# Padding between the split ffn inputs in their pool, and one parameter tile moved to another pool

## The chip, the cores and the metric

The kernel runs on one core of one Trainium2 chip. Its time is the device time of one execution in microseconds (us). A core has a matrix engine (TensorE; PE in the profile, with its weight loads as PEld), three engines for elementwise work (VectorE, DVE; ScalarE, ACT; GpSimd, POOL), a queue engine (SyncE, SP) and DMA engines that move data between the main memory and the on-chip memory. On-chip memory (SBUF) has 128 partitions; a tile takes the same byte range in each partition, and this text speaks of addresses as bytes within a partition. Matmul results go to PSUM tiles of at most 512 float32 columns.

## The reference

Two layers over 1024 latent tokens and 256 context tokens, model width 1024, all float32. Each layer is a mixer and a channel mixer (ffn), each behind a modulated RMS norm and with a gated residual. The mixer of layer 0 is attention beside a convolution, that of layer 1 a recurrent scan in both directions. What the change touches are the inputs of the last two products of each layer:

```python
def swiglu(h, w1, w3, w2):
    return (jax.nn.silu(h @ w1) * (h @ w3)) @ w2
...
        h_lat = h_lat + g1_l * o_lat
        f_lat = rms_norm(h_lat, norm_ffn[i]) * (1 + sc2_l) + sh2_l
        h_lat = h_lat + g2_l * swiglu(f_lat, ffn_w1[i], ffn_w3[i], ffn_w2[i])
        if not last:
            h_ctx = h_ctx + g1_c * o_ctx
            f_ctx = rms_norm(h_ctx, norm_ffn[i]) * (1 + sc2_c) + sh2_c
            h_ctx = h_ctx + g2_c * swiglu(f_ctx, ffn_w1[i], ffn_w3[i], ffn_w2[i])
```

`o_lat` is the output of the mixer, itself a product with a 1024 by 1024 matrix (`even_w_out`, `rw_wo`). The ffn's hidden width is 2816, and context tokens go through it in layer 0 only.

## The kernel before

**Split products.** Every large product is done in three matmuls of float32r, a float32 format that TensorE reads at one pass: an operand is split into a rounded part (`hi`) and the rest (`lo`), and `mm3` (line 57) adds `wh·xh`, `wh·xl` and `wl·xh` on lines 59, 60 and 61. In a call to matmul the second argument is the stationary operand (128 by 128, loaded into the array by a weight load) and the third is the moving one (128 by up to 512 columns). A weight load of the next matmul goes on while the matmul before it streams its moving operand.

**Tokens.** They are tiled as `TT`: 256 context tokens (tile 0) and two tiles of 512 latent tokens (1 and 2). In layer 1 only two tiles of 512 remain (0 and 1).

**The split inputs.** `operands` (line 1446) opens a pool `X0` or `X1` on the left side of SBUF and puts into it, tile after tile, `xh` and `xl`: eight blocks (kb) of 128 features, each a run of 256 or 512 tokens. Layer 0 has the order 1, 0, 2 and layer 1 the order 0, 1. The same tiles serve twice: first they hold the split output of the mixer, which `mix_out` (line 680) multiplies with the output projection into PSUM tiles `pw`; then `norm_split` writes the split input of the ffn into them.

**The ffn** (line 718) runs over 22 blocks of 128 hidden features in groups of two. For each block and token tile, two PSUM tiles `pf` (for w1 and w3) take 8 × 3 = 24 matmuls each, moving `xh`/`xl` past the stationary `whi`/`wlo`. The product of the two goes, split again, to `gh`/`gl`, and then eight PSUM tiles `pf2` for each token tile take 2 × 3 = 6 matmuls, moving `gh`/`gl` past the rows of w2, which lie in tiles of the same names `whi`/`wlo`. ACT and DVE split the weights (lines 54 and 55) and finish the results (lines 750, 751 and 762) meanwhile.

**Where tiles lie.** Pools on the left stack upwards, with the pool `G` of constants and parameters at the bottom (its last byte is at 22,176 before the change); pools with `side="right"` stack downwards from the top of the partition. A pool's tiles lie in the order in which they are made. Added up from the tile sizes, before the change:

| tile | pool, side | address | mod 512 |
|---|---|---|---|
| `ah` (inputs of layer 0's projections `pg`, `pz`) | A0, left | 22,176 | 160 |
| `whi` for them | W0, left | 108,192 | 160 |
| `xh1`, `xh0`, `xh2`, layer 0 | X0, left | 22,176, 54,944, 71,328 | 160 |
| `whi`, layer 0 projection and ffn | WX0 and FW0, right | 155,616 and 151,520 | 480 |
| `gh`, layer 0 | FW0, right | 112,608 | 480 |
| `xh0`, `xh1`, layer 1 | X1, left | 42,080, 74,848 | 96 |
| `wyh0` (first two blocks of layer 1's projection) | WY, left, above X1 | 110,688 | 96 |
| `whi`, layer 1 projection and ffn | WX1 and FW1, right | 156,576 and 152,480 | 416 |
| `gh`, layer 1 | FW1, right | 119,712 | 416 |

The `lo` tiles and the further buffers lie whole multiples of 512 bytes away from these; so do the kb blocks (2048 bytes of `xh` for 512 tokens, 1024 for 256; 512 of `whi`). A pool that is opened over a closed one reuses its bytes, and its first writers wait for the last readers of the old tiles below them.

**X1 opens early.** `prepared` (line 1484) opens X1 while the scan of layer 1 still runs, in the place of the scan's preparation pool (`prep`), loads six of the eight blocks of each x tile through `o` (`layer1_in`, line 1408), and starts the projection's first two output blocks with the early weights `wyh`/`wyl`.

**`rt`** is a tile of 128 by 128 (512 bytes) into which `params` (line 108) collects parameter rows, group by group (A, B, C, M), before a transposition puts them into `parA` to `parM`. It lies in `G`, with one buffer. T0 is the right-hand pool of the first stage, closed when the inputs are normed; T1, also on the right, takes its place later with `zq2`.

Of the kernel before, what the change touches and what calls it, by code (L numbers as in the profile page):

```python
# [9 lines left out]
F32 = mybir.dt.float32  # L10
F32R = mybir.dt.float32r
# [6 lines left out]
P = 128  # L18
D = 1024
KB = D // P  # L20
# [19 lines left out]
def f32(ap):  # L40
    return ap.bitcast(F32)


class Kern:
# [60 lines left out]
        self.Wr = None  # L105
        self.acc = {}

    def params(self, *groups):

        nc, tc, I = self.nc, self.tc, self.I  # L110
        rows = {
            "A": ["c", "c_ctx", "ada_b", "norm_mix"],
            "B": ["mla_q_norm", "mla_kv_norm", "conv_b", "conv_ln_g", "conv_ln_b", "rw_k_k", "rw_k_a",
                  "rw_w0", "rw_a0", "rw_r_k", "rw_ln_g", "rw_ln_b", "norm_ffn"],
            "C": ["conv_w"],
            "M": ["rw_mu"],
        }
        for g in groups:
            rt = self.G.tile([P, P], F32, tag="rt", name="rt", bufs=1)
            nc.vector.memset(rt, 0.0)  # L120
            r = 0
            where = {}
            for nm in rows[g]:
                a = I[nm]
                n = int(np.prod(a.shape)) // P
                sh = list(a.shape)
                if len(sh) == 1:
                    a2 = a.rearrange("(b p) -> b p", p=P)
                elif len(sh) == 2:
                    a2 = a.rearrange("a (b p) -> (a b) p", p=P)  # L130
                elif len(sh) == 3:
                    a2 = a.rearrange("a c (b p) -> (a c b) p", p=P)
                elif nm == "rw_r_k":
                    a2 = a.rearrange("a c (h e) d -> (a c h) (e d)", e=2)
                else:
                    a2 = a.rearrange("a c e (b p) -> (a c e b) p", p=P)
                (nc.sync if g == "A" else nc.gpsimd).dma_start(rt[r:r + n, :], a2)
                where[nm] = (r, n)
                r += n
            ps = self.psM.tile([P, 512], F32, tag="m", name="ps")[:, :P]  # L140
            nc.tensor.transpose(ps, rt, self.ident)
            ct = self.G.tile([P, P], F32, tag="par" + g, name="par" + g)
            nc.vector.tensor_copy(ct, ps)
            for nm, (r, n) in where.items():
                self.par[nm] = ct[:, r:r + n]
            if g == "A":
                nc.scalar.activation(self.silc[:, :, 0], self.par["c"], AF.Silu)
                nc.scalar.activation(self.silc[:, :, 1], self.par["c_ctx"], AF.Silu)
# [95 lines left out]
    def layer0_mix(self):  # L244
# [6 lines left out]
        with ExitStack() as st:  # L251
            pool = lambda s, **k: s.enter_context(tc.tile_pool(reuse_waits="tile", **k))
# [5 lines left out]
            A = pool(left, name="A0", bufs=1)  # L258
# [3 lines left out]
            self.W, self.wraw, self.wbuf = W, 1, 2  # L262

            with tc.tile_pool(name="T0", bufs=1, side="right", reuse_waits="tile") as tp:
                self.params("A")
                xs = []
                ss = tp.tile([P, NTK], F32, name="ss")

                def load(b, q):
                    x = tp.tile([P, D], F32, tag="xin" if b < 2 else "araw", name="xin", bufs=2 if b < 2 else 18)  # L270
                    r = b * P
                    q.dma_start(x, I["ctx"][0][r:r + P] if r < NCTX else I["x"][0][r - NCTX:r - NCTX + P])
                    xs.append(x)

                def rms(b0, b1):
                    for b in range(b0, b1):
                        sq = tp.tile([P, D], F32, tag="sq", name="sq", bufs=1)
                        nc.scalar.activation(sq, xs[b], AF.Square, accum_out=ss[:, b:b + 1])
                    r = ss[:, b0:b1]
                    nc.scalar.activation(r, r, AF.Sqrt, bias=self.eps, scale=1.0 / D)  # L280
                    nc.vector.reciprocal(r, r)
                    for b in range(b0, b1):
                        nc.vector.tensor_scalar(xs[b], xs[b], ss[:, b:b + 1], None, op0=ALU.mult)

                for b in range(2):
                    load(b, nc.sync)
                for _ in self.ada(0, 0, 2, tp, 18, psO, psM):
                    pass
                w0 = [self.load_w(w_in[:, c0:c0 + P]) for c0 in (544, 1056)]
                for b in range(2, NTK):  # L290
                    load(b, nc.sync)
                rms(0, 2)
                self.gains(0, 0)
                for t0, n in TT:
                    if t0:
                        rms(t0 // P, (t0 + n) // P)
                    for g in {256: "BC", 768: "M"}.get(t0, ()):
                        self.params(g)
                    s = int(t0 == 0)
                    for fb in range(KB):  # L300
                        ps = psM.tile([P, 512], F32, tag="m", name="tps")
                        for i in range(n // P):
                            nc.tensor.transpose(ps[:, i * P:(i + 1) * P], xs[t0 // P + i][:, fb * P:(fb + 1) * P], self.ident)
                        t = tp.tile([P, 512], F32, tag="nt", name="nt", bufs=3)
                        nc.scalar.activation(t[:, :n], ps[:, :n], AF.Identity, scale=self.gs[:, 0, 0, s, fb:fb + 1], bias=self.mod[0][:, fb, s:s + 1])
                        hi = ah[:, fb, t0:t0 + n]
                        nc.gpsimd.tensor_scalar(hi, t[:, :n], 1.0, 0.0, op0=ALU.mult, op1=ALU.add)
                        nc.vector.tensor_tensor(al[:, fb, t0:t0 + n], t[:, :n], f32(hi), op=ALU.subtract)
# [68 lines left out]
            with tc.tile_pool(name="T1", bufs=1, side="right", reuse_waits="tile") as tp:  # L377
                ada = self.ada(0, 2, 6, tp, 3, psO, psM)
                for j in range(4):
# [5 lines left out]
                    g = self.par["mla_q_norm" if j < 2 else "mla_kv_norm"][:, j % 2:j % 2 + 1]  # L385
# [252 lines left out]
            for i in range(NH):  # L638
# [11 lines left out]
                for j, _ in enumerate(attend(i)):  # L650
                    for sd in side:
                        g, n, a, b, d = sd
# [784 lines left out]
    def run(self):  # L1437
        tc = self.tc
        pool = lambda s, **k: s.enter_context(tc.tile_pool(reuse_waits="tile", **k))
        with ExitStack() as st:  # L1440
# [5 lines left out]
            def operands(l, sizes):  # L1446
                X = pool(xs, name=f"X{l}", bufs=1)
                order = (0, 1) if l else (1, 0, 2)
                xs_ = {i: [X.tile([P, KB, sizes[i]], F32R, name=f"x{k}{i}") for k in "hl"] for i in order}
                xh, xl = ([xs_[i][k] for i in range(len(sizes))] for k in range(2))  # L1450
                return order, xh, xl, pool(ps, name=f"pX{l}", bufs=5, space=PSUM)

# [23 lines left out]

            sizes = [n for _, n in TT]
            hT = phase(0, sizes, operands(0, sizes), self.layer0_out)
            LR = pool(rs, name="LR", bufs=1)
            self.layer1_proj(hT, hs.close, LR)  # L1480
            nn.close()
            sizes, x = [512, 512], []

            def prepared():
                x.extend(operands(1, sizes))
                _, xh, xl, psum = x
                self.x1 = xh, xl
                Y = pool(ys, name="WY", bufs=1)
                self.wy = []

                def load(mb):
                    w = [Y.tile([P, KB, P], F32R, name=f"wy{k}{mb}") for k in "hl"]
                    for k0, k1 in ((0, 6), (6, 8)):
                        raw = self.wyr[:, :k1 - k0]
                        self.nc.sync.dma_start(raw, self.I["rw_wo"][0][k0 * P:k1 * P, mb * P:(mb + 1) * P].rearrange("(k p) m -> p k m", p=P))
                        self.split(w[0][:, k0:k1], w[1][:, k0:k1], raw)
                    self.wy.append(w)

                self.wyr = Y.tile([P, 6, P], F32, name="raw")
                load(0)  # L1500
                with tc.tile_pool(name="TY", bufs=1, reuse_waits="tile") as tp:
                    self.layer1_in(xh, xl, tp)
                yield
                Y = pool(ys, name="WZ", bufs=1)
                load(1)
                for mb in range(2):
                    w = self.wy[mb]
                    for ti in range(2):
                        ps = self.acc[mb, ti] = psum.tile([P, 512], F32, tag="mm", name="pw")
                        for kb in range(6):  # L1510
                            self.mm3(ps, w[0][:, kb], w[1][:, kb], xh[ti][:, kb], xl[ti][:, kb], kb == 0, False)
                            if kb % 3 == 2:
                                yield
# [55 lines left out]
```

## Time and profile before

| | us |
|---|---|
| three runs, median (lowest to highest) | 4186.94 (4185.19 to 4190.39) |
| the profiled execution | 4188.13 |
| its span, first to last instruction | 4186.4 |
| TensorE busy | 3832.1 |
| DVE busy | 2403.9 |
| ACT busy | 1741.1 |
| POOL busy | 1161.3 |

The profile is of one execution. "PE" rows are matmuls and "PEld" rows weight loads, which overlap them; matmuls are pipelined, so the duration of one (from its start to its modelled end) is longer than the step from one start to the next. The granted clock is the share of TensorE's full clock that the chip allowed at the time. Names stand without their trailing numbers: `xh0`, `xh1` and `xh2` are all `xh`, and `gh` is the source that tells `pf2` from `pf`.

### The profile page before, as it was taken

To read this page: it belongs to the slowest core of one execution; us is meant where nothing else is said; L and a number is where in the kernel's file an instruction comes from. 1 tells how busy PE (TensorE), PEld (TensorE's weight loads), DVE (VectorE), ACT (ScalarE), POOL (GpSimd) and SP (SyncE) were. 2 spreads that over 40 slices of the span, in tenths; PEclk is the share of its full clock that TensorE was granted. 3 is DMA by queue.
4 is the path that set the end of the run, shared out by engine and by line. 5 is a ranking of instruction groups with operands and counts; after the bars stand their busy time and mean duration, and the time that the engine had idled before them with its cause. 6 is when DMAs were issued, how large, how long until landed. Compare 5 with 4: busy or idle time off the path is not lost. (4 is left out here: it accounts for less than half of the span.)

```text
span 4186.4 us, 70705 instructions
## 1 busy us (share of the span) xinstructions
PE 3832.1 (92%) x28764; PEld 3132.3 (75%) x28764; DVE 2403.9 (57%) x4577; ACT 1741.1 (42%) x3590; POOL 1161.3 (28%) x978
## 2 busy tenths in 40 slices
PE   8888899899999999997998979787887799999999
PEld 5665667688888888886887957676776578888887
DVE  5698776555333433338678378878787654333433
ACT  4446566643111111116667357666666442111111
POOL 2869554510000000004223164645544020000000
PEclk9898999999999999998999979898988899999999
DMA  4322222331111111113223222222222231111111
GB/s 174 125 86 69 74 92 72 109 109 46 41 39 33 40 41 41 36 36 99 74 95 102 79 85 70 80 70 78 75 62 65 85 111 51 46 45 51 51 46 56
DMA packets 301669, 297.07 MB, mean 71 GB/s; under 512 B 19408, under 2 KB 267872, under 8 KB 301344
## 3 DMA queue, kind: packets, MB, share of 16 engines
q1 hardware_dynamic: 293488, 277.07, 21.4%
q10 hardware_dynamic: 7056, 14.75, 1.0%
q8 instruction: 227, 3.72, 0.4%
q0 software_dynamic: 800, 0.73, 0.1%
q14 instruction: 98, 0.80, 0.1%
HBM read 246.36 MB, written 46.14 MB: 70 GB/s over the span
## 5 line engine op out<-in xcount | busy, mean ns | idle before, releaser
L59 PE MATMUL pf<-xh,whi 128*128 128x512 f32 (+1 forms) x1760 | 654.2, 372 | 0.0
L61 PE MATMUL pf<-xh,wlo 128*128 128x512 f32 (+1 forms) x1760 | 654.1, 372 | 0.0
L60 PE MATMUL pf<-xl,whi 128*128 128x512 f32 (+1 forms) x1760 | 653.8, 372 | 0.0
L54 ACT ACTIVATE whi<-raw 128x1024 fp32r<-128x1024 f32 (+1 forms) x207 | 214.8, 1049 | 909.3 <-PE pf L60 788.5
L55 DVE TENSOR_TENSOR wlo<-raw,whi 128x1024 fp32r<-128x1024 f32 (+1 forms) x207 | 270.1, 1314 | 259.6 <-ACT whi L54 254.9
L762 DVE SCALAR_TENSOR_TENSOR hT<-pf,mod,hT 128x512 f32<-128x512 f32 (+1 forms) x440 | 306.3, 697 | 196.3 <-PE pf L61 194.3
L751 DVE TENSOR_TENSOR sl<-sl,pf 128x512 f32<-128x512 f32 (+1 forms) x110 | 69.8, 635 | 581.2 <-PE pf L61 581.2
L61 PEld LDWEIGHTS pf<-xh,wlo 128*128 128x128 f32 x1760 | 330.8, 188 | 64.7
L60 PEld LDWEIGHTS pf<-xl,whi 128*128 128x128 f32 x1760 | 330.8, 188 | 64.5
L59 PEld LDWEIGHTS pf<-xh,whi 128*128 128x128 f32 x1760 | 330.6, 188 | 64.6 <-ACT xh L221 0.3
L60 PE MATMUL pf<-gl,whi 128*128 128x512 f32 (+1 forms) x880 | 324.1, 368 | 0.0
L61 PE MATMUL pf<-gh,wlo 128*128 128x512 f32 (+1 forms) x880 | 323.9, 368 | 0.0
L59 PE MATMUL pf<-gh,whi 128*128 128x512 f32 (+1 forms) x880 | 323.9, 368 | 0.0
L581 POOL TENSOR_TENSOR pl<-pe,pt 128x512 fp32r<-128x512 f32 (+1 forms) x176 | 226.4, 1297 | 190.8 <-PE po L60 103.0
L791 POOL MEMSET apad<- 128x8 f32 x4 | 0.2, 122 | 884.6 <-PE pf L61 884.6
L367 POOL TENSOR_TENSOR co<-co,cpr 128x655 f32<-128x655 f32 x90 | 193.8, 2154 | 46.6 <-ACT cpr L366 36.9
L54 ACT ACTIVATE gh<-sl 128x512 fp32r<-128x512 f32 (+1 forms) x110 | 64.9, 590 | 307.8 <-DVE sl L751 307.8
L59 PEld LDWEIGHTS pf<-gh,whi 128*128 128x128 f32 x880 | 165.9, 189 | 27.9
L60 PEld LDWEIGHTS pf<-gl,whi 128*128 128x128 f32 x880 | 165.9, 189 | 27.7
L61 PEld LDWEIGHTS pf<-gh,wlo 128*128 128x128 f32 x880 | 165.9, 189 | 27.6
L1203 DVE TENSOR_TENSOR tmp<-A,X 128x126 f32<-128x126 f32 (+22 forms) x620 | 154.0, 248 | 52.3 <-ACT X L1197 38.6
L354 DVE SCALAR_TENSOR_TENSOR co<-yp,parC,co 128x1310 f32<-128x1310 f32 (+1 forms) x90 | 177.0, 1967 | 1.5
(407 smaller groups left out, 9634.8 us busy)
## 6 DMA issues: line engine op xcount, KB each, us to landing
raw<-in_ffn_w_dram SPq DMA_DIRECT2D x132, 512.0 KB, 3.9
araw<-in_ada_w_dram SPq DMA_DIRECT2D x96, 512.0 KB, 4.5
low<-lod SPq DMA_DIRECT2D x40, 256.0 KB, 2.8
kw<-kd SPq DMA_DIRECT2D x40, 256.0 KB, 3.0
kkw<-kkd SPq DMA_DIRECT2D x40, 256.0 KB, 2.8
sv<-vd SPq DMA_DIRECT2D x80, 128.0 KB, 3.1
raw<-in_even_w_out_dram SPq DMA_DIRECT2D x16, 512.0 KB, 3.6
rw<-rd SPq DMA_DIRECT2D x32, 256.0 KB, 3.1
```

Source lines behind the costliest of these rows:

```text
L54: self.nc.scalar.activation(hi, src, AF.Copy)
L55: return self.nc.vector.tensor_tensor(lo, src, f32(hi), op=ALU.subtract)
L59: mm(ps, wh, xh, start=start, stop=False)
L60: mm(ps, wh, xl, start=False, stop=False)
L61: mm(ps, wl, xh, start=False, stop=stop)
L354: nc.vector.scalar_tensor_tensor(co, yp[:, w + c:w + c + n], cw(j, w), co, op0=ALU.mult, op1=ALU.add)
L367: nc.gpsimd.tensor_tensor(co, co, pr, op=ALU.add)
L581: nc.gpsimd.tensor_tensor(pl, pe, f32(pt), op=ALU.subtract)
L751: nc.vector.tensor_tensor(sl[:, :n], sl[:, :n], pp[1][:, :n], op=ALU.mult)
L762: nc.vector.scalar_tensor_tensor(hT[ti][:, mb], ps[:, :n], g[:, mb], hT[ti][:, mb], op0=ALU.mult, op1=ALU.add)
L791: nc.gpsimd.memset(ap[:, :, c:c + 1], 0.0)
L1203: nc.vector.tensor_tensor(tmp, A[:, k + 1:32, k:k + 1].to_broadcast([P, n, wd]), X[:, k:k + 1, 0:wd].to_broadcast([P, n, wd]), op=ALU.mult)
```

## The change

`rt` is made in the pool that the caller hands to `params`, which is T0, no longer in `G`. And `operands` lays unused tiles between the split inputs, counted in floats of four bytes: `at` is the offset from the start of the pool, a tile of 512 tokens is put at an offset of 80 mod 128 floats, and the tile of 256 tokens at one of 128 mod 256 floats.

```diff
-    def params(self, *groups):
+    def params(self, pool, *groups):
...
-            rt = self.G.tile([P, P], F32, tag="rt", name="rt", bufs=1)
+            rt = pool.tile([P, P], F32, tag="rt", name="rt", bufs=1)
...
-                self.params("A")
+                self.params(tp, "A")
...
-                        self.params(g)
+                        self.params(tp, g)
...
                 order = (0, 1) if l else (1, 0, 2)
-                xs_ = {i: [X.tile([P, KB, sizes[i]], F32R, name=f"x{k}{i}") for k in "hl"] for i in order}
+
+                xs_, at = {}, 0
+                for i in order:
+                    pad = (80 - at) % 128 if sizes[i] == 512 else (128 - at) % 256
+                    if pad:
+                        X.tile([P, pad], F32, name=f"pad{i}")
+                        at += pad
+                    xs_[i] = []
+                    for k in "hl":
+                        xs_[i].append(X.tile([P, KB, sizes[i]], F32R, name=f"x{k}{i}"))
+                        at += KB * sizes[i]
                 xh, xl = ([xs_[i][k] for i in range(len(sizes))] for k in range(2))
```

## The prediction

> **What bounds the kernel now.** I read the page first, then the table of stretches, then the groups by form, and last the starts of single matmuls. The page (its span, the TensorE row, the granted clock by slice, and the row of the chain that ended last, by line):
>
> ```profile
> span 4186.4 us, 70705 instructions
> PE 3832.1 (92%) x28764; PEld 3132.3 (75%) x28764; DVE 2403.9 (57%) x4577; ACT 1741.1 (42%) x3590; POOL 1161.3 (28%) x978
> ...
> PEclk9898999999999999998999979898988899999999
> ...
> PE pf L59 6%; PE pf L61 6%; PE pf L60 6%; DMA out_dram<-o 0%; PE t L1429 0%; PE cps L186 0%; ACT o L1431 0%; PE cpb L193 0%; DVE hT L762 0%; ACTq L1431 0%
> ```
>
> TensorE is busy for 92% of the span, and the end of the chain is the three matmuls of `mm3` (lines 59 to 61). A mean over a kernel of many stages proves little, so here are the stretches in which the split inputs are used: output projection of layer 0, its ffn, output projection of layer 1, its ffn. A row gives length, then busy time and count of PE, PEld, DVE, ACT and POOL, granted clock, DMA share and GB/s.
>
> ```profile
> 840.00:968.00 128.00, 122.44 (x643) 102.99 (x641) 67.81 (x107) 54.01 (x89) 15.71 (x12) 0.97 0.29 89
> 968.00:1892.00 924.00, 923.25 (x4799) 784.47 (x4800) 345.69 (x508) 161.77 (x246) 16.13 (x22) 1.00 0.13 40
> 3300.00:3434.00 134.00, 120.45 (x770) 92.63 (x767) 72.54 (x131) 49.25 (x96) 20.95 (x15) 0.93 0.42 123
> 3434.00:4170.00 736.00, 735.93 (x3188) 596.24 (x3186) 280.15 (x363) 131.66 (x177) 4.56 (x3) 1.00 0.15 46
> ```
>
> Both ffn stretches, 1660 us together, are filled by TensorE at full clock, with every other engine under 40% busy and DMA at 13 to 15%. There a matmul that takes its place for less time shortens the kernel one for one. The waits agree; over the ffn of layer 0 this is the only wait of TensorE's matmuls, and over that of layer 1 there is none:
>
> ```profile
> PE cps L186 <- POOL sq L208: 2.9, 1, 2.9
> ```
>
> **What a matmul costs at which distance.** "Distance" is the address of the moving operand minus that of the stationary one, mod 512 bytes. All strides of one kb are multiples of 512, so it is one number per pair of tiles. From the address table: `xh`/`xl` against `whi`/`wlo` of the ffn and of the projections is 192, for all tiles; `gh`/`gl` against the ffn's weights 0; `ah`/`al` against `whi` 0; `xh`/`xl` against `wyh`/`wyl` 0. Matmuls are pipelined, so their price is the step from start to start. I took stretches that hold one kind of matmul only:
>
> ```profile
> 307.30:322.97 15.67, 15.67 (x71) 1.00 0.00 0
> 866.85:872.21 5.36, 5.36 (x25) 1.00 0.33 98
> 1112.40:1123.30 10.90, 10.90 (x49) 1.00 0.17 49
> 1123.30:1129.05 5.75, 5.75 (x49) 1.00 0.01 3
> 1151.16:1156.61 5.45, 5.45 (x49) 1.00 0.00 0
> 1156.61:1179.01 22.40, 22.40 (x98) 1.00 0.17 48
> 3381.14:3400.51 19.37, 19.37 (x84) 1.00 0.38 108
> 3503.50:3548.30 44.80, 44.80 (x193) 1.00 0.19 59
> 3548.30:3570.08 21.78, 21.78 (x97) 1.00 0.09 25
> ```
>
> The count includes one or two matmuls of the group before that still drain; the code's own numbers (24 to a PSUM tile in `pf`, 6 in `pf2`) give the divisor. The profile drops digits at the end of names, so `pf2` stands as `pf` there, with `gh` or `gl` as its source. In order:
> - `pg<-ah`, 512 wide, distance 0: 15.67/69 = 227.1 ns
> - `pw<-xh`, layer 0, 512, distance 192: 5.36/23 = 233.0
> - `pf2<-gh`, layer 0, 512, distance 0: 10.90/48 = 227.1
> - `pf2<-gh`, 256 wide, distance 0: 5.75/48 = 119.8
> - `pf<-xh`, 256 wide, distance 192: 5.45/48 = 113.5
> - `pf<-xh`, layer 0, 512, distance 192: 22.40/96 = 233.3
> - `pw<-xh`, layer 1, 512, distance 192: 19.37/83 = 233.4
> - `pf<-xh`, layer 1, 512, distance 192: 44.80/192 = 233.3
> - `pf2<-gh`, layer 1, 512, distance 0: 21.78/96 = 226.9
>
> So 512 columns cost 6.2 to 6.4 ns less at distance 0 than at 192, and 256 columns 6.3 ns more. The clock is 1.00 in every row. What remains is whether the distance does it, or something else that differs between `pf` and `pf2` (group length, tile stride). Two rows speak for the distance. `pg` has groups of 24, and its tiles are laid out kb by kb as `xh` is; it runs at 227. And the same `xh`/`xl` tiles, against weights that lie at distance 0, give (start, duration; eleven steps lie between these two rows, no other work among them):
>
> ```profile
> 3333.37 0.39 PE L59 MATMUL pw<-xh,wyh 128*128 128x512 f32 x1
> ...
> 3335.86 0.39 PE L61 MATMUL pw<-xh,wyl 128*128 128x512 f32 x1
> ```
>
> 2.49/11 = 226.4 ns. That is the changed state of the disputed matmul, already in this trace.
>
> One rule of the Trainium skill speaks against all this: SBUF — State Buffer, section "Who interferes with whom", gives PE two independent read ports, one for the moving operand and one for the weight load, and says that PE waits on nobody. By that rule an address would not matter and the sum would be 0; the rows above, 233.3 against 227.1 and 226.4 at equal width and clock, disagree with it.
>
> **The change part by part.**
>
> (1) *Where the tiles go.* `rt` leaves G: everything on the left stack sinks by 512 bytes, which changes no distance. `X0` then begins at 21,664; 80 floats put `xh1` at 21,984, and 21,984 − 151,520 = −253 × 512, distance 0. With its two tiles the pool is at 8,272 floats; 48 more bring `xh0` to 54,944, distance 192 as before; 80 more bring `xh2` to 71,648, distance 0. In layer 1 the first 80 floats put `xh0` at 41,888, distance 0, and `xh1` needs none. Right-hand pools hang from the top and don't move. The pool `WY` moves with X1, so `wyh` stays at 0.
>
> (2) *The ffn.* Counts by form, layer 0 and then layer 1 (line, engine, names, form, count, busy us, mean ns); `mm3` issues lines 59, 60 and 61 once each, so every count is to be taken three times:
>
> ```profile
> L59 PE MATMUL pf<-xh,whi 128*128 128x512 f32 x704 | 278.5, 396 | 0.0
> L59 PE MATMUL pf<-gh,whi 128*128 128x512 f32 x352 | 137.2, 390 | 0.0
> L59 PE MATMUL pf<-xh,whi 128*128 128x256 f32 x352 | 97.3, 277 | 0.0
> ```
> ```profile
> L59 PE MATMUL pf<-xh,whi 128*128 128x512 f32 x704 | 278.4, 395 | 0.0
> L59 PE MATMUL pf<-gh,whi 128*128 128x512 f32 x352 | 137.0, 389 | 0.0
> ```
>
> 2112 matmuls of 512 in each layer. Layer 0: 2112 × (233.3 − 227.1) = 13.1 us. Layer 1: 2112 × (233.3 − 226.9) = 13.5 us. The 256-wide ones and `pf2` keep their distance: 0. Sum 26.6 us, all of it on the path. Nothing is late next: DVE has 345.69 us of work in 924, DMA a share of 0.13.
>
> (3) *The output projections* read the same tiles:
>
> ```profile
> L61 PE MATMUL pw<-xh,wlo 128*128 128x512 f32 x128 | 51.8, 405 | 0.0
> ```
> ```profile
> L61 PE MATMUL pw<-xh,wlo 128*128 128x512 f32 x96 | 38.7, 405 | 0.0
> ```
>
> 3 × 128 + 3 × 96 = 672 matmuls at 192; 672 × 6.2 = 4.2 us. TensorE is idle 5.6 us in the first of these stretches and 13.6 in the second, so some of it may fall into waits: between 0 and 4.2. I take 4.2, since the stretches above show them back to back.
>
> (4) *Pads and `rt`.* The pads are never written or read; they cost room (320 bytes on the left in layer 0, net) and change which old tiles a new one covers. In layer 0 no x tile covers an old tile that it did not cover before. In layer 1 `xh0` now also covers a `kw` buffer, and `xl0` covers `srk`. Last readers of those, then the first writers of the x tiles (count, duration, first and last start):
>
> ```profile
> L1056 POOL TENSOR_TENSOR t<-t,kw x40: 1262/1278/1717, 2374.5 to 3225.0; 128x512 f32<-128x512 f32 x40
> L1188 PE MATMUL cfp<-cq,srk x128: 379/403/637, 2495.9 to 3278.2; 128*32 128x256 f32 x128
> ```
> ```profile
> L54 ACT ACTIVATE xh<-o x12: 617/630/632, 3299.5 to 3323.8; 128x512 fp32r<-128x512 f32 x12
> ```
>
> 3225 and 3278 lie 21 us or more before 3299: the added waits are over when they are asked. They'd sit on ACT and DVE, ahead of the other splits; a late one would cost its lateness. `rt` in T0 keeps its one buffer and its order; its place is taken next by `zq2` of pool T1 (`zq` in the profile):
>
> ```profile
> L141 PE MATMUL ps<-ident,rt x4: 275/374/446, 6.8 to 57.5; 128*128 128x128 f32 x4
> ```
> ```profile
> L392 ACT ACTIVATE zq<-pz x12: 363/576/583, 120.3 to 260.2; 128x512 f32<-128x512 f32 x8, 128x256 f32<-128x256 f32 x4
> ```
>
> 58 is over before 120: nothing. No DMA is added and no queue is passed.
>
> Sum: 13.1 + 13.5 + 4.2 = 30.8 us. The profiled execution took 4188.13 us (1.7 around its span), so it would take 4157.3; the median shown, 4186.94, is 1.2 lower and gives **4156**.
>
> **Bounds.** The step of 512 columns has rows from 226.4 to 227.1 at distance 0, and from 233.0 to 233.4 at 192: a gain of 5.9 to 7.0 each. 4224 × 5.9 = 24.9 us with nothing from the projections; 4896 × 7.0 = 34.3 with all 672 of theirs. Against the median: 4152.6 to 4162.0; the three runs shown reach 1.8 below it and 3.5 above, so 4151 to 4166.
>
> **The rivals.**
> - *Half a change* (0.06): only one layer's pools land where the sums put them, or new waits after the shift give back a dozen us: some 13 to 17 us gained, about 4172. Against it: both layers' addresses and the 21 us of slack.
> - *No change* (0.05): the distance is a bystander and `pf` has its 233 from something else, or the weights move along with the inputs: 0 us, so 4187. For it speaks only that `pf` never ran at 0; against it, `xh` at 226.4 beside `wyh`. The Trainium skill's rule of independent ports, quoted above, would bring this out.
> - *Slower* (0.02): distance 0 is the dear one, as it is for the 256-wide rows (119.8 against 113.5), and `pf2` and `pg` are quick for another reason. All 4896 of them, 4224 in the ffn and 672 in the projections, × 6.3 = +30.8 us: 4218. It decides as soon as a 512-wide step at 0 exceeds 233.3. Against it: every 512-wide row at distance 0 is under 228.
> - *More* (0.02): everything beyond the columns themselves goes. At distance 0, 256 more columns cost 227.1 − 119.8 = 107.3 ns, so 512 bare ones would cost 214.6; 4896 × 18.7 = 92 us: 4095. No row shows a step under 226. The Trainium skill's page TensorE: Matmul & The Clock Gate, section "Back-to-back issue gap", would have 512 columns at N/2.4 + 2.5 = 215.8 ns, an estimate that no stretch here reaches.
>
> **How the numbers follow.** The forecast has 0.85 with its own bounds, 4151 to 4166; the rivals outside hold 0.15, so the range needs no more. A measurement of this kernel tells 0.2% (8.4 us) from no change. Faster: 0.85 + 0.06 + 0.02 = 0.93; same 0.05; slower 0.02.
>
> **What would show it.** The same stretches: `pf` 512 wide at 227 ns a step instead of 233.3 and its mean duration at 390 instead of 396; 256 wide unchanged at 113.5 and 277; the ffn of layer 0 911 us long instead of 924, that of layer 1 722.5 instead of 736; `pw` at 227. The prediction is wrong if `pf` keeps 233, or if the steps shrink and another stretch grows: the start of layer 1's output projection (3300 on) is the place to look first.

## The result, and the profile after

| | before, us | after, us |
|---|---|---|
| median (lowest to highest) of four runs each | 4186.06 (4177.46 to 4190.39) | 4155.10 (4154.82 to 4161.12) |
| the profiled execution | 4188.13 | 4161.12 |

The ratio is 0.993, with a 95% interval of 0.9917 to 0.9942; 4156 was forecast. Here is the page of the changed kernel, its span and the row of the engines:

```profile
span 4159.4 us, 70715 instructions
PE 3807.0 (92%) x28764; PEld 3142.4 (76%) x28764; DVE 2397.4 (58%) x4577; ACT 1739.4 (42%) x3590; POOL 1164.9 (28%) x978
```

The count of matmuls is unchanged, and so is the order of the work on every engine, but for a few pairs that start within a fraction of a us of each other (the ten instructions more only handle semaphores): the 27 us between the two profiled executions come out of durations, not out of another program. The table of stretches of the changed kernel, for the two ffn:

```profile
966.00:1880.00 914.00, 913.54 (x4797) 788.48 (x4798) 345.41 (x508) 161.01 (x245) 15.65 (x22) 1.00 0.13 40
3420.00:4143.30 723.30, 723.30 (x3190) 598.85 (x3190) 280.06 (x363) 132.21 (x179) 4.26 (x3) 1.00 0.16 47
```

As before, TensorE fills both, at full clock. They were 924 and 736 us long; now the same work takes 914 and 723. Stretches that hold one kind of matmul (length, busy time and count of PE, clock, DMA share, GB/s), in the order 256-wide `pf` at distance 192; 512-wide `pf` of layer 0 and of layer 1, now at 0; and `pf2` of layer 1, which lay at 0 all along:

```profile
1146.91:1152.56 5.65, 5.65 (x49) 1.00 0.00 0
1152.56:1174.32 21.76, 21.76 (x98) 1.00 0.17 49
3490.07:3533.59 43.52, 43.52 (x193) 1.00 0.20 60
3533.59:3555.35 21.76, 21.76 (x97) 1.00 0.09 25
```

Divided by 48, 96, 192 and 96 matmuls: 117.7, 226.7, 226.7 and 226.7 ns. The 512-wide `pf` do what was forecast (233.3 before), and can't be told from `pf2` any more. The 256-wide ones do not: their addresses are the same byte for byte (`xh0` at 54,944 in both kernels, the weights unmoved), and yet a step takes 117.7 ns and not 113.5. The groups by form of the ffn of layer 0 say the same in durations (396 and 277 ns before):

```profile
L59 PE MATMUL pf<-xh,whi 128*128 128x512 f32 x704 | 274.3, 390 | 0.0
...
L59 PE MATMUL pf<-xh,whi 128*128 128x256 f32 x352 | 98.9, 281 | 0.0
```

Where the time went, from the first to the last start of each stage's matmuls in the two profiles:

| stage | before, us | after, us | difference | forecast |
|---|---|---|---|---|
| output projection, layer 0 | 121.8 | 118.9 | −2.9 | |
| ffn, layer 0 | 921.6 | 912.0 | −9.6 | −13.1 |
| output projection, layer 1, from the first matmul at the moved distance | 83.9 | 82.8 | −1.1 | −4.2 for both projections |
| ffn, layer 1 | 735.6 | 722.4 | −13.2 | −13.5 |
| sum | | | −26.8 | −30.8 |

The profiled executions differ by 27.0 us, so the four stages account for it. The medians differ by 31.0; some 4 us of that no stage shows. The runs of the kernel before alone are spread over 13 us.

### The profile page after: what moved, and what is told of

It reads as the page before. It is cut to its first block, busy times and chain, and to the rows that moved or that the text cites. A ratio compares the mean times of both kernels' runs of the same rounds, so it can differ in the third digit from the quotient of the medians.

```text
span 4159.4 us, 70715 instructions
## 1 busy us (share of the span) xinstructions
PE 3807.0 (92%) x28764; PEld 3142.4 (76%) x28764; DVE 2397.4 (58%) x4577; ACT 1739.4 (42%) x3590; POOL 1164.9 (28%) x978
```

## The experiments

Two questions were open. Does the distance mod 512 bring the gain, and nothing else of the change? And why did the 256-wide matmuls, whose addresses did not move, become slower? The theory for the second: a run of 256-wide matmuls has more than one stable rhythm (a step from start to start that repeats), and keeps the one that it takes over from the run ahead of it. The rival: a part of the change that was costed at nothing (the left stack, 512 bytes lower, or `rt`) slows them.

### The parts of the change alone

All of these kernels, and those of the next two sections, keep the whole of the change but for one line in `operands`, which takes the distance of each tile from a table:

```diff
-                    pad = (80 - at) % 128 if sizes[i] == 512 else (128 - at) % 256
+                    pad = (({0: {1: 192, 0: 192, 2: 192}, 1: {0: 192, 1: 192}}[l][i] - 192) // 4 - at) % 128
```

As shown, every tile stays at 192 and only `rt` moves (`rt_only`). With 0 for tiles 1 and 2 of layer 0 it is `layer0_only`, with 0 for both tiles of layer 1 `layer1_only`. Expected:

> All x tiles stay at distance 192; only rt is moved, so that the left stack sinks by 512 bytes. If the distance mod 512 does it all: no change (ratio 1.000 within 0.001), pf 512 wide at 233.3 ns a step and 256 wide at 113.5. If the sunk stack or rt is what raised the 256-wide step of the changed kernel from 113.5 to 117.8: 117.8 here too, and about 5 us more than before (1248 x 4.3 ns).

> Layer 0 as in the change, layer 1 at distance 192. If the distance does it: pf 512 wide of layer 0 at 227 (2112 x 6.6 ns = 13.9 us) and pw (384 x 6.3 = 2.4), less 1248 x 4.3 = 5.4 us for the 256-wide ones at 117.8: about 10.9 us less than before, ratio 0.9974; layer 1's pf at 233.3. If the gain of layer 0 is bought by something in the start of the kernel: nothing like that sum.

> Layer 1 as in the change, layer 0 at distance 192. If the distance does it: 2112 x 6.6 + 288 x 6.3 ns = 15.7 us less than before, ratio 0.9962, and the two halves together give the whole. If the early projection pays for new neighbours below X1: less than 14 us, with the loss between 3250 and 3420 us. The 256-wide steps of layer 0 stay at 113.5.

Measured, on one chip against the same runs of the kernel before (median 4184.04 us):

| | median, us | ratio to before (95% interval) | ffn of layer 0, us | ffn of layer 1, us | 256-wide step, ns |
|---|---|---|---|---|---|
| `rt_only` | 4181.00 | 0.9998 (0.9985 to 1.001) | 921.7 | 735.6 | 113.6 |
| `layer0_only` | 4169.90 | 0.9974 (0.9964 to 0.9985) | 912.3 | 736.1 | 117.8 |
| `layer1_only` | 4162.75 | 0.9960 (0.9945 to 0.9974) | 921.6 | 722.4 | 113.5 |

The ratios are those on record; they are not the quotients of the medians, which would be 0.9993, 0.9966 and 0.9949. Expected were 0.9974 for `layer0_only`, which came to the fourth digit, and 0.9962 for `layer1_only`, well inside its interval, and each shortens its own ffn alone. Moving `rt` does nothing that can be measured, and it leaves the 256-wide steps at 113.4 to 113.6 in 20 of 21 unbroken runs, so the rival falls: neither the sunk stack nor `rt` is it. (The step in the table is that of the middle one of these runs; the one that differs is looked at below.) They slow down exactly where the 512-wide tiles around them, in layer 0, lie at 0. The groups by form in the ffn of layer 1 show `layer0_only` where the kernel before was:

```profile
L59 PE MATMUL pf<-xh,whi 128*128 128x512 f32 x704 | 278.7, 396 | 0.0
```

### The run ahead of the 256-wide one

`entry` puts tile 1 of layer 0 back to 192, the tile that runs just ahead of the 256-wide one in the order 1, 0, 2, and leaves tile 2 at 0:

```diff
-                    pad = (80 - at) % 128 if sizes[i] == 512 else (128 - at) % 256
+                    pad = (({0: {1: 192, 0: 192, 2: 0}, 1: {0: 64, 1: 128}}[l][i] - 192) // 4 - at) % 128
```

> In layer 0 the tile that runs ahead of the 256-wide one (xh1) goes back to 192, xh0 stays at 192 and xh2 is at 0. Theory of the entered mode: a 256-wide run keeps the rhythm in which the run ahead leaves the array, so it is back at 113.5. Rival, that something else of the change costs the 4.3 ns (the sunk left stack, rt, the pads): 117.8 again. In layer 1 xh0 lies at 64 and xh1 at 128, distances that no clean stretch shows: between 226 and 234 ns if 0 and 192 are the ends; a step outside these would say that the rows so far did not show the whole range.

Single-kind stretches of it: the 256-wide run, then `xh0` and `xh1` of layer 1 at 64 and at 128:

```profile
1149.71:1155.16 5.45, 5.45 (x49) 1.00 0.00 0
3704.59:3715.59 11.00, 11.00 (x49) 1.00 0.31 95
3715.59:3726.75 11.16, 11.16 (x49) 1.00 0.16 46
```

48 matmuls each: 113.5, 229.2 and 232.5 ns. The 256-wide run is back at its old step, with `rt`, the pads and the low stack all in place. What it depends on is the run ahead. (The kernel took 4185.92 us in its one run. Its two ffn were still shorter than before, 915.2 and 731.7 us, but its scan took 889.9 us against 884.2.)

The trace of before shows this too. In its first ffn group the matmuls of a norm cut a 256-wide run in two; behind them the same run goes on in the other rhythm, at distance 192 and in a kernel without pads:

```profile
986.37:989.91 3.54, 3.54 (x33) 1.00 0.00 0
```

30 steps in 3.54 us are 118 ns. And in `rt_only`, where every tile lies at 192, one unbroken 256-wide run of the first group has the slow rhythm, behind a 512-wide run at 192:

```profile
1005.79:1011.44 5.65, 5.65 (x49) 1.00 0.00 0
```

48 matmuls, 117.7 ns. The steps of the 512-wide run ahead alternate between 231 and 236 ns. It ends with one of 231; ahead of the other 20 runs of `rt_only`, and of all 21 of before, the last step was 233 to 236. So what is passed on is the rhythm of the run ahead, which its distance alone does not fix. The entry itself can be read in the starts of single matmuls. First the kernel before, then the changed one, at the same place in the output projection (start, duration):

```profile
872.27 0.40 PE L61 MATMUL pw<-xh,wlo 128*128 128x512 f32 x1
872.50 0.28 PE L59 MATMUL pw<-xh,whi 128*128 128x256 f32 x1
872.62 0.28 PE L60 MATMUL pw<-xl,whi 128*128 128x256 f32 x1
872.74 0.28 PE L61 MATMUL pw<-xh,wlo 128*128 128x256 f32 x1
872.85 0.28 PE L59 MATMUL pw<-xh,whi 128*128 128x256 f32 x1
```
```profile
862.89 0.39 PE L61 MATMUL pw<-xh,wlo 128*128 128x512 f32 x1
863.12 0.28 PE L59 MATMUL pw<-xh,whi 128*128 128x256 f32 x1
863.24 0.28 PE L60 MATMUL pw<-xl,whi 128*128 128x256 f32 x1
863.35 0.28 PE L61 MATMUL pw<-xh,wlo 128*128 128x256 f32 x1
863.47 0.28 PE L59 MATMUL pw<-xh,whi 128*128 128x256 f32 x1
```

Behind a run at 192 the first step is long and then they are short (from 872.62 on, 0.113 on average); behind a run at 0 they stay at 0.117 to 0.119, for all 24 or 48 of them.

### Other distances

Four kernels with the same line and other tables: layer 0 (tiles 1, 0, 2) and layer 1 (tiles 0, 1) at 0, 256, 320 and 256, 384 (`scan_a`); at 0, 64, 448 and 32, 480 (`scan_b`); at 0, 384, 160 and 416, 96 (`scan_c`); at 0, 448, 224 and 288, 352 (`scan_d`).

> Distances: layer 0 xh1 0, xh0 (256 wide) 256, xh2 320; layer 1 xh0 256, xh1 384. If the step of 512 columns falls with the overlap of the two address ranges in the 512-byte cycle, it rises from 227 at 0 over 229.1 at 64 to 232.4 at 128 and 233.3 at 192 and falls back on the other side of 256: 256 at 233 or more, 320 at 233, 384 at 232. If 0 is one of several good places, one of them is at 227 or below. The 256-wide run follows a run at distance 0: 117.8 if the entered mode alone counts, another value if its own distance counts too.

> Distances: layer 0 xh1 0, xh0 (256 wide) 64, xh2 448; layer 1 xh0 32, xh1 480. By the overlap: 32 between 227 and 229, 480 and 448 the same as 32 and 64 if the cycle is symmetric about 0. If only the direction forward counts: 448 and 480 near 233. The 256-wide run at 64: between 117.8 and 119.8 by the entered mode, 113.5 or less if it has a good place there.

> Distances: layer 0 xh1 0, xh0 (256 wide) 384, xh2 160; layer 1 xh0 416, xh1 96. By the overlap: 96 between 229.1 and 232.4, 160 between 232.4 and 233.3. The 256-wide run at 384: looked at for a place that stays at 113.5 or below although the run ahead is at 0; 117.8 if there is none.

> Distances: layer 0 xh1 0, xh0 (256 wide) 448, xh2 224; layer 1 xh0 288, xh1 352. By the overlap: all three 512-wide ones at 232 to 234. The 256-wide run at 448: as in scan_c. If no distance beats 0 for 512 columns, and one beats 117.8 for 256 behind a run at 0, then the two together are a version quicker than the change by up to 1248 x 4.3 = 5.4 us.

Steps between starts in clean runs of `pf`, ns:

| distance | 0 | 32 | 64 | 96 | 128 | 160 | 192 | 224 | 256 | 288 | 320 | 352 | 384 | 416 | 448 | 480 |
|---|---|---|---|---|---|---|---|---|---|---|---|---|---|---|---|---|
| 512 wide | 226.7 to 227.6 | 233.4 | 229.2 | 233.2 | 232.5 | 234.2 | 233.3 | 233.3 | 226.7 to 227.0 | 233.3 | 233.4 | 233.3 | 233.2 | 234.2 | 233.3 | 233.2 |
| 256 wide, behind a run at 0 | | | 117.8 | | | | 117.8 | | 119.8 | | | | 119.9 | | 117.8 | |

The row of 256 in the stretches of `scan_a` (48 matmuls), and that of 32 in those of `scan_b`:

```profile
3696.25:3707.13 10.88, 10.88 (x49) 1.00 0.30 96
```
```profile
3697.42:3708.63 11.21, 11.21 (x49) 1.00 0.30 94
```

226.7 and 233.5 ns. The overlap theory of the expectations (the step falls with the overlap of the two address ranges) falls: 32 is as dear as 192. What is left is a narrow good place at 0 and a second one at 256, which the overlap theory did not have, with 64 as a half-good one. No distance beats 0 for 512 columns, and none of the five tried for 256 columns gets below 117.7 behind a run at 0. The 226.7 at 0 rises to as much as 227.6, as a mean over 48 matmuls, behind a run at another distance. Most distances were seen behind one or two kinds of run only, and rhythms are inherited, so an entry of this table is not a constant of its distance. The four kernels had one run each, 4175.65 to 4181.79 us beside one of 4176.94 of the kernel before; that says nothing about their order.

### Breaking the rhythm, and the same padding in another stage

`kick_p3m` halves one matmul near the start of the 256-wide run, in a cycle over the hidden blocks: none; the run's second one in 2 × 128; of the run ahead, the last but one, or the last, in 2 × 256. In the first stage of layer 1 it also pads the mixed inputs `mh`/`ml` (256 wide, at distance 0 from `whi`) to 192:

```diff
...
+                            cuts = [(0, n)] * 3
+                            if kick == 1 and ti == 0 and w is w13[i][0] and kb == 0:
+                                cuts[1] = (0, 128)
+                            if kick in (2, 3) and ti == 1 and w is w13[i][1] and kb == KB - 1:
+                                cuts[kick - 1] = (0, 256)
...
             M = pool(st, name="M3", bufs=1)
+            M.tile([P, 48], F32, name="padm")
             W = pool(st, name="W3", bufs=1)
+            W.tile([P, 80], F32, name="padw")
```

> The changed kernel with two more edits. (1) In the ffn of layer 0, block by block in a cycle of four: untouched; the second matmul of the 256-wide run in two of 128 columns; the last but one matmul of the 512-wide run ahead of it in two of 256; the last of that run in two of 256. If the 256-wide run keeps the rhythm that it is entered with, at least one of these three sends it back to 113.5 ns a step while the untouched blocks stay at 117.8; if its step is fixed by the addresses, all four stay at 117.8. (2) In the first stage of layer 1, mh/ml lie at distance 192 from whi instead of 0, so that the 256-wide matmuls p3m (1728) go from 120.0 to between 113.5 and 117.8, and p3v (480, 512 wide, now at 320) from 227.1 to 233.4: between 4 and 11 us less, and 3 us more. Whole kernel: 0 to 9 us less than the change, so 4146 to 4155 where the change has 4155, ratio to before 0.991 to 0.993. If what was read off the ffn does not carry over to another stage: p3m stays at 120 and the kernel is 3 us slower than the change.

Its 256-wide runs from the seventh matmul on, in the order of the cycle (42, 40, 42 and 44 steps):

```profile
1141.21:1146.15 4.94, 4.94 (x44) 1.00 0.00 0
1168.96:1173.49 4.53, 4.53 (x42) 1.00 0.00 0
1223.53:1228.29 4.76, 4.76 (x44) 1.00 0.00 0
1250.54:1255.53 4.99, 4.99 (x46) 1.00 0.00 0
```

117.6, then 113.3, 113.3 and 113.4 ns. Each of the three disturbances sends the run back into the quick rhythm, and the untouched blocks stay in the slow one, in one kernel with one set of addresses. Halving the last matmul ahead costs next to nothing: its halves take 113 and 119 ns, together 6 more than the whole. The kernel's median was 4141.29 us, ratio 0.9904 (0.9882 to 0.9927). That is some 5 us below the 4146 to 4155 that were expected, and not all of it is the work of the edits. Beside `change_again` (below), its profiled execution took 14 us less: 1.9 of that lie in the ffn of layer 0, 5.2 between the first `p3m` and the first matmul of the scan, and 6.2 in the output projection of layer 1, which the edits leave alone. That stage ran at a granted clock of 0.97 here and of 0.93 there.

`both` uses that halving ahead of every 256-wide run, in the ffn and the output projection of layer 0, with the pads in M3 and W3; `change_again` is the change on the same chip:

```diff
...
-        mm(ps, wl, xh, start=False, stop=stop)
+        if halves:
+            mm(ps[:, :256], wl, xh[:, :256], start=False, stop=False)
+            mm(ps[:, 256:], wl, xh[:, 256:], start=False, stop=stop)
+        else:
+            mm(ps, wl, xh, start=False, stop=stop)
...
+                                     not l and ti == 1 and w is w13[i][1] and kb == KB - 1)
```

> The change itself once more, for a comparison on the chip on which the next kernel runs: ratio to before 0.993 (0.991 to 0.995), 256-wide steps at 117.8 ns, p3m at 120.

> The change, with the last 512-wide matmul ahead of every 256-wide run (ffn and output projection of layer 0) issued as two of 256 columns, and mh/ml at distance 192 from whi. All 256-wide runs of layer 0 at 113.7: 1248 x 4.1 ns = 5.1 us; p3m at 113.3 instead of 120: 1728 x 6.7 = 11.6 us where the stage waits for TensorE, p3v at 229 to 233: 480 x 2 to 6 = 1 to 3 us back. 13 to 16 us less than the change on the same chip, ratio to before 0.990. If the first edit's gain needed the mixture of blocks: 117.8 in some runs and 10 to 11 us.

`change_again`: 4155.15 us, 0.9929 (0.9913 to 0.9945). `both`: 4156.12 us, 0.9937 (0.9923 to 0.9951): no gain, where 13 to 16 us had been expected. The stages ahead of the scan did most of what was expected: the ffn of layer 0 took 908.6 us against 912.0, and the scan's first matmul (`abp`) started at 2387.1 us against 2397.4. By the start of the early projection, at 3281.0 against 3281.6, the lead was gone. With the added matmuls, the scan's instructions stand in another order than in the change, on all engines. To see whether that is the cause, `pads_only` drops the halving and keeps the pads of M3 and W3; its order is that of the kernel before.

> The change, and mh/ml at distance 192 from whi; no matmul is added, so every engine's instructions come in the order of the kernel before. p3m 1728 x 6.7 ns less = 11.6 us where its stage waits for TensorE (about 2000 to 2390 us), p3v 480 x 2 to 6 ns back: the start of the scan 8 to 10 us earlier than in the change. Theory that the kernel with halved matmuls lost its gain to the other order of the scan: here the scan keeps its length, and the kernel takes 4145 to 4147 us, ratio 0.9905 to 0.991. Rival, that the scan gives back any earlier start (something else paces its end): 4155, ratio 0.993.

4151.19 us (4147.43 to 4156.69), 0.9922 (0.9910 to 0.9934): between the 4145 to 4147 of the theory and the 4155 of its rival. A stretch of `p3m` in the changed kernel, and the same one here:

```profile
2302.00:2350.00 48.00, 48.00 (x402) 1.00 0.16 54
```
```profile
2302.00:2350.00 48.00, 48.00 (x426) 1.00 0.21 69
```

120 ns a matmul before, 113 now (two of each count still drain). But its 512-wide `p3v`, in two runs at one and the same distance, takes 229 ns in the first and 233 in the second (34 matmuls each):

```profile
2150.13:2157.93 7.80, 7.80 (x36) 1.00 0.10 34
2199.95:2207.88 7.93, 7.93 (x36) 1.00 0.11 35
```

From the first `p3m` to the first `abp` it took 501.9 us against 506.9, a gain of 5 where 8 to 10 were expected; from there to the early projection, the scan, 878.8 against 884.3 in `change_again` and 893.9 in `both`. That fits the theory of the order, but doesn't settle it: executions with one and the same order had scans from 876.2 (`scan_c`) to 889.9 us (`entry`). Much of that scatter goes with the granted clock of the scan: 876.2 to 880.7 us at 0.88, 881.2 to 884.5 at 0.87, 889.9 at 0.86. At the same clock the two kernels with added matmuls, both in another order, were longer: `both` with 893.9 us at 0.87, `kick_p3m` with 884.7 at 0.88. With one profiled execution of each, that stays a hint. Nor do the intervals of 0.9922 and 0.9929 tell `pads_only` from the change. `kick_p3m` has the lowest ratio, 0.9904, but it ran on another chip, its interval overlaps that of the change, and much of its lead lies in a stage that it doesn't touch; so no version here is shown to beat the change.

## Why the prediction was right

- *The layout* (its part 1) came out to the byte: `xh1` at 21,984, `xh0` at 54,944, `xh2` at 71,648, `xh0` of layer 1 at 41,888.
- *The 512-wide steps* (part 2): 227.1 and 226.9 were taken from `pg` and `pf2`; 226.7 came. The three witnesses at distance 0, above all `xh` beside `wyh` at 226.4, were worth their lines. Layer 1's ffn: 13.5 forecast, 13.2 measured.
- *"The 256-wide ones and `pf2` keep their distance: 0"* is the step that failed. It held for `pf2`; the 256-wide `pf` gave back 1056 × 4.2 ns = 4.4 us, and layer 0's ffn gained 9.6 instead of 13.1. The step took the price of a matmul as a function of its own addresses. The runs showed that it also depends on the run ahead of it.
- *The projections* (part 3): 4.2 forecast, 4.0 in the two profiles. That of layer 0 has 192 matmuls of 256 columns that lost some 4 ns each, too; in `change_again` the stage gained only 1.6 us (121.8 to 120.2). That of layer 1 took 85.7 us in `change_again`, more than the 83.9 of before: its length goes with its granted clock, from 79.5 us at 0.97 (`kick_p3m`) to 85.7 at 0.93. So this term is not known better than to some 2 us, and that it came out at 4.0 is partly luck.
- *Pads and `rt` at nothing* (part 4): the ratio of `rt_only` is 0.9998 (0.9985 to 1.001), and no stage outside the four differs by over 2 us between the two profiles.
- *The sum* was 30.8, and the stages gained 26.8. The forecast median was met within 1 us because the two medians lie 31.0 apart, 4 more than the stages show; on the chip of `change_again` they lie 26.7 apart (4181.83 and 4155.15). Part of that closeness is luck.
- *The rivals.* "No change" and "slower" fell with the first stretch of `pf`, "half a change" with the gains of both ffn, and "more" because no run of 512-wide `pf` at 0 had a step under 226.6 ns on average. "Slower" had a grain: the 256-wide ones did get slower, though not at distance 0. By the Trainium skill's SBUF — State Buffer, "Who interferes with whom", the two read ports of PE are independent; here the step of equal matmuls at clock 1.00 goes from 226.7 to 234.2 ns with nothing moved but the distance of the two operands, so in this kernel the measurement speaks against what the prediction drew from the rule, that an address would not matter.

## What to carry to other kernels

Where a stage is filled by float32r matmuls, take the step from start to start, sort it by width and by the distance of the two operands' addresses, and look for a pair of tiles that lies better already: that row is the price of a padding before it is built. Price the neighbours of the moved tiles too, since a run can inherit its rhythm, and a few halved matmuls between two runs are a cheap way to test that. Compare stage by stage, with the granted clock of each: 5 us in one stage disappear in the scatter of a scan that varies by 14.

## What the runs showed of the hardware

- The step of a 512-wide float32r matmul depends on where the moving operand lies relative to the stationary one, in a cycle of at most 512 bytes. For `pf` it was 226.7 ns at 0 (up to 227.6 behind a run at another distance), 226.7 to 227.0 at 256, 229.2 at 64, and 232.5 to 234.2 at the other thirteen multiples of 32.
- 256-wide ones have two stable steps at one distance, 113.5 and 117.7 ns at 192. Which one a run takes depends on the matmuls just ahead of it or on a foreign one near its start; it shows within the first six steps, and no run of `pf` left it afterwards without a foreign matmul in between.
- 512-wide ones can have two as well: 229 and 233 ns for `p3v` at distance 320, in one execution.
- Why the array behaves so was not tried; the runs show where the steps are, not what in the memory or the array makes them.
